# Holding the grams and the merges of inverses for a place behind a scan step on TensorE

## The chip, the cores and the metric

The kernel runs on one core of a Trainium2 chip. The metric is the device time of one execution in microseconds; the kernel before has a median of 1652.41 us over three runs. The core has five engines with a queue each: TensorE (PE, with its weight loads as PEld), VectorE (DVE), ScalarE (ACT), GpSimd (POOL) and SyncE (SP, which here only issues transfers).

## The reference

Two samples of 512 tokens and width 1024 pass through two layers with shared weights. Layer 0 is a bidirectional RWKV-7 time mixing with 16 heads of 64; layer 1 is a neighbourhood attention. Cut to what matters here:

```python
r, k, v = heads(lerp(0) @ w_r), heads(lerp(1) @ w_k), heads(lerp(2) @ w_v); z = xn @ w_z
for d in range(2):                       # forward and backward
    ...                                  # decay, a, k_d from two low-rank products
    def step(s, inp):                    # 512 steps of it, in order or reversed
        sa = einsum('bhvk,bhk->bhv', s, a_t)
        s = s * w_t + sa[..., None] * b_t + v_t[..., None] * k_t
        return s, einsum('bhvk,bhk->bhv', s, r_t)
    ys.append(scan(step, ...))
y = ys[0] + ys[1]                        # normed per head, bonus added, times silu(z), @ w_o
x = x + rms(y @ w_o)                     # then the layer of attention in the same frame
```

## The kernel before

The recurrence is done in chunks of 64 tokens (`NCH` = 8 a sequence). The work is cut into eight **blocks** (`self.todo`): two samples by four groups of four heads. For each block:

- `prep` (twice a block, for a pair of heads each, two directions d) makes the decays and the tile `ab`, and then a **gram** for each d: one bunch of 32x2 small f32 matmuls of 64x32 tiles (L975) into the bank `pf`. ScalarE copies it to Gd and Go (L981). `prep` goes on only when the gram of the direction before it has issued.
- `inverse` makes the inverse of 64x64 unit triangular matrices, 32 at a time: 32x32 halves by elimination on VectorE (L1011 transposes in, L1018 and L1020 are 30 pairs of dependent operations, L1022 masks, L1028 and L1033 transpose out to NA and MT), and then the **merges** of the halves on TensorE: two bunches of 32x32 tiles at L1049 and two at L1051, each in a bank `pm`, each followed by ScalarE copies back to NA (L1056) or MT (L1059).
- eight **scan steps** (`step`, a burst of some 55 us): states (L1186, L1192), solve and factors (L1213, L1092, L1114) and outputs (L1233, L1237), all in tiles of 64x64 or 128x64.
- `finish` norms y and stores it.

Beside the blocks runs a long list of **products** (L826 to L828): full 128x128 tiles, 24 matmuls for a column of 128 outputs, for r, v, k, z, then w_o of sample 0 (which needs the finish of sample 0's four blocks) and w_in of layer 1. Their weights and operands are split in two parts by ScalarE and VectorE (L745, L747, L771, L773).

The order of TensorE, VectorE and ScalarE in this stage is written at build time by a planner, `weave`: every activity is a thread (a generator) that yields the engine it wants next, a gate and a function `needs` that says from which time on its next piece can run. `Clock` keeps a model of the time. `weave` takes, among the threads whose time has come, the one with the lowest rank: steps 0, prep 1.5, posts 2, inverse 5, products 9. If nothing can run and TensorE has been idle, it issues a warming matmul (L1643). A thread that waits holds up itself alone, not the engine's queue. `Clock.mode` is the tile size of the last planned matmul; a change of tile size costs 100 ns in the model. The inverses are one thread, block after block:

```python
for n, (s, pb) in enumerate(self.todo):
    yield "D", lambda: did["preps"] > n and did["steps"] >= NCH * (n - 1)
    yield from self.inverse(s, pb)
    did["inverse"] += 1
```

and the second part of a step waits with `did["inverse"] > st.n`. The functions that the change touches:

Of the kernel before, what the change touches and what calls it, by code (L numbers as in the profile page):

```python
# [19 lines left out]
P = 128  # L20
# [30 lines left out]
class Clock:  # L51
# [40 lines left out]
    def room(self, key, bufs):  # L92
        s = self.slots.get(key, ())
        return 0.0 if len(s) < bufs else min(self.left(n) for n in s)

    def at(self, names):

        return max([max(self.made.get(n, {}).values(), default=0.0) for n in names], default=0.0)
# [133 lines left out]
class Trunk:  # L232
# [20 lines left out]
    NZ1, STOCK, EPS, NEAR = 4, 1, 60.0, 400.0  # L253
    HACT = (3, 4)
    WARM = 300.0
    AHEADE = dict(S=3000.0, A=200.0, D=200.0)

    def __init__(self, ctx, tc, a):
# [59 lines left out]
    def bank(self, tag="pm"):  # L318

        return (lambda: self.clock.room(tag, self.bufs[tag]) < 1e11), (lambda c: max(c.room(tag, self.bufs[tag]), 0.0))  # L320

    def dram(self, tag, shape=(P, T)):
        return self.dp.tile(list(shape), F32, tag=tag, name=self.name("d" + tag))
# [523 lines left out]
    def prep(self, s, p):  # L847
# [6 lines left out]
        need = lambda *xs: lambda c, n=[x.tensor.name for x in xs]: c.at(n)  # L854
# [33 lines left out]
        free, room = self.bank()  # L888
        for d in range(2):
# [36 lines left out]
            ab = b("ab", (P, NCH, 4, L), 1)  # L926
# [34 lines left out]
            def gram(ab=ab, d=d):  # L961

                free, room = self.bank("pf")
                yield "P", free, lambda c: max(room(c), need(ab)(c))
                ps = self.p("pf", (P, 2, T))[:, :, 0:4 * L].rearrange("p h (i t) -> p h i t", i=4)
                for i2 in range(4):
                    for par in range(2):
                        for hf in range(2):
                            for h in range(2):
                                e, i = (par + d) % 2, 2 * i2 + par  # L970
                                q = 64 * e + 32 * hf
                                rhs = ab[half(h), i, 1 if e else 2]
                                if hf:
                                    rhs = rhs.rearrange("p (b t) -> p b t", b=2)[:, ::-1]
                                nc.tensor.matmul(  # L975
                                    ps[q:q + 32, h, i2], ab[half(h), i, 3 if e else 0, 32 * hf:32 * hf + 32], rhs,
                                    start=True, stop=True, tile_position=(64 * h, q))
                yield "A", None, need(ps)
                for par in range(2):
                    e = (par + d) % 2  # L980
                    act.copy(Gd[half(e), :, par::2, g], ps[half(e), :, :, 0:32])  # L981
                    act.copy(Go[half(e), :, par::2, g], ps[half(e), :, :, 32:64])

            grams = gram()

        yield from grams
# [12 lines left out]
    def inverse(self, s, pb):  # L999

        nc = self.nc
        vt, gps, act = nc.vector, nc.gpsimd, nc.scalar
        f = lambda tag, shape: self.t(tag, shape, 1, F32, self.front)
        wc, Gd, Go = self.formed[s, pb]
        NU = 32
        free, room = self.bank()
        need = lambda *xs: lambda c, n=[x.tensor.name for x in xs]: c.at(n)
        gd, go = (x.rearrange("p h i g t -> p (h i g) t") for x in (Gd, Go))
        yield "D", None, need(Gd)
        N = f("N", (P, 32, 32))  # L1010
        vt.transpose(N, gd.rearrange("p u t -> p t u"))  # L1011
        tmp = f("etmp", (P, 256))
        self.did["gd"] += 1
        for q in range(1, 31):
            n = 31 - q
            tv = tmp[:, :n * q].rearrange("p (i j) -> p i j", i=n)
            yield "D"
            vt.tensor_tensor(tv, N[:, q + 1:, q:q + 1].broadcast_to([P, n, q]), N[:, q:q + 1, :q].broadcast_to([P, n, q]), op=ALU.mult)  # L1018
            yield "D"
            vt.tensor_tensor(N[:, q + 1:, :q], tv, N[:, q + 1:, :q], op=ALU.add)  # L1020
        yield "D"
        vt.tensor_tensor(N, N, self.lower, op=ALU.mult)  # L1022
        yield "D"
        vt.memset(N.rearrange("p i j -> p (i j)")[:, 0:1024:33], 1.0)

        yield "D"
        NA = f("NA", (P, NU, 32))
        vt.transpose(NA.rearrange("p u j -> p j u"), N.rearrange("p i j -> p j i"))  # L1028
        MT = self.MTb[self.nM % 2]
        self.nM += 1  # L1030

        yield "D"
        vt.transpose(MT[:, :, 0, :].rearrange("p u i -> p i u"), N)  # L1033
        yield "A"
        for q in (1, 3):
            r = slice(32 * q, 32 * q + 32)
            act.copy(MT[r, :, 1], MT[r, :, 0])
            gps.memset(MT[r, :, 0], 0.0)
        for step in range(2):
            for j0 in (0, 16):  # L1040
                us = slice(j0, j0 + 16)
                yield "P", free, (lambda c: max(room(c), need(NA)(c))) if step == 0 else (lambda c: max(room(c), need(MT)(c)))
                ps = self.p("pm", (P, 16, 32))
                for j in range(16):
                    for h in range(2):
                        x, y = slice(64 * h, 64 * h + 32), slice(64 * h + 32, 64 * h + 64)
                        u = j0 + j
                        if step == 0:
                            nc.tensor.matmul(ps[y, j], go[x, u], NA[x, u], start=True, stop=True, tile_position=(64 * h, 64 * h + 32))  # L1049
                        else:  # L1050
                            nc.tensor.matmul(ps[x, j], NA[y, u], MT[y, u, 1], start=True, stop=True, tile_position=(64 * h + 32, 64 * h))  # L1051
                yield "A", None, need(ps)
                for h in range(2):
                    if step == 0:
                        y = slice(64 * h + 32, 64 * h + 64)
                        act.copy(NA[y, us], ps[y])  # L1056
                    else:
                        x = slice(64 * h, 64 * h + 32)
                        act.copy(MT[x, us, 1], ps[x])  # L1059
        self.formed[s, pb] = wc, MT  # L1060
# [60 lines left out]
    def alone(self, q):  # L1121

        did, st = self.did, self.steps[q]
        free, room = self.bank("pf")
        bank, here = self.bank()
        yield (
            "P", lambda: did["factors"] > q or (did["fetch"] > q and (did["solve"] >= q if q else bank()) and free()),
            lambda c: 0.0 if did["factors"] > q else max(c.at([st.ab.tensor.name]), room(c), 0.0 if q else here(c)))
        if did["factors"] == q:
            self.factors(q)  # L1130
# [486 lines left out]
    def weave(self, threads):  # L1617

        ck, did = self.clock, self.did
        while True:  # L1620
# [5 lines left out]
            for t in ts:  # L1626
# [5 lines left out]
                else:  # L1632
                    late = max(at - max(now, ck.t[t.eng]) - self.EPS, ck.t[t.eng] - now - self.AHEADE[t.eng])
                if late <= 0:
# [3 lines left out]
                else:  # L1638
                    wake.append(now + late)
                    if t.eng == "P":  # L1640
                        soon.append(late)
            if best is None and self.spare is not None and ck.cool(now) and min(soon, default=1e9) > self.WARM:
                self.nc.tensor.matmul(self.spare, self.ident, self.scan[0][:, 0:256], start=not did["states"], stop=True, skip_group_check=True)  # L1643
# [14 lines left out]
    def scan_phase(self, mid):  # L1658
# [61 lines left out]
        def each(f):  # L1720
# [4 lines left out]
            Thread(lambda: 0, each(self.step)), Thread(lambda: 0.5, each(self.alone)), Thread(lambda: 0.5, each(self.near)),  # L1725
            Thread(lambda: 1, each(self.outer)),
            Thread(lambda: 0, fetch()), Thread(lambda: 0, fetch_x()), *self.flow(), Thread(lambda: 5, inverse()), Thread(lambda: 1.5, preps()),
            Thread(lambda: 1.3 if did["finish"] == 3 else 4, finish()), Thread(lambda: 1.2, self.norm0(0))]
        e = mybir.EngineType
# [202 lines left out]
```

## Time and profile before

| | |
|---|---|
| runs | 1654.68, 1652.41, 1652.31 us; median 1652.41 |
| the profiled execution | span 1657.8 us from the first to the last instruction; no other time of it is listed |
| PE / PEld busy | 1558.3 us (94%) / 1195.6 us (72%) |
| DVE / ACT / POOL busy | 1218.7 us (74%) / 1013.3 us (61%) / 177.9 us (11%) |
| products in this stage, L826 + L827 + L828 | 284.7 + 258.1 + 257.2 us busy |
| grams L975 / merges L1049, L1051 | 29.1 us (x2048) / 19.9 and 21.1 us (x1024 each) |
| warming matmuls L1643 | 52.9 us (x200) |

Matmuls overlap in the pipeline, so sums of busy time over groups exceed the time that they take; intervals between starts say more. In the windows view each row is a stretch of the span: its length, then for PE, PEld, DVE, ACT and POOL the busy time and the count of instructions, then the granted TensorE clock, the share of the DMA engines and GB/s; restricted to a line it shows only the engines that this line uses. In the timeline each row is a start, a time, an engine, the line, the operation, the tiles written and read, shapes and a count of merged instructions, and in brackets idle time before it with its releaser.

### The profile page before, as it was taken

What the parts mean: (1) busy time and instruction counts of PE and PEld (TensorE: products, weight loads), DVE (VectorE), ACT (ScalarE), POOL (GpSimd) and SP (SyncE); (2) the same over time, 40 slices, a digit from 0 to 9 for tenths busy, and PEclk for the clock granted to TensorE, in tenths of its full rate; (3) what the DMA queues carried; (4) which work ended last, traced back from release to release, by engine and by line L of the source; (5) the groups of instructions that cost most, each with busy time, mean ns of one, the idle gap of its engine ahead of it and who ended that gap; (6) DMA issues with size and microseconds to landing.
All of it is one profiled execution on the core that took longest, in us unless ns stands there. A gap on an engine that the chain in (4) does not pass through costs nothing.

```text
span 1657.8 us, 46551 instructions
## 1 busy us (share of the span) xinstructions
PE 1558.3 (94%) x18824; PEld 1195.6 (72%) x18824; DVE 1218.7 (74%) x2711; ACT 1013.3 (61%) x2025; POOL 177.9 (11%) x338
## 2 busy tenths in 40 slices
PE   7989888898999998988988999999999999999998
PEld 5867667676767776766766767777777778777776
DVE  8886668688789687886879887855677585665564
ACT  6567656766765677655665765354567665455562
POOL 0000213411101123000000111000000002100000
PEclk9999999999999899988988999999999999999999
DMA  5455578676687687664668665554765346745453
GB/s 212 157 174 175 183 259 283 212 233 224 211 257 253 193 265 255 220 219 162 222 218 266 205 227 188 185 178 129 286 216 179 109 140 206 246 159 182 163 163 103
DMA packets 176184, 336.29 MB, mean 203 GB/s; under 512 B 20928, under 2 KB 53824, under 8 KB 175968
## 3 DMA queue, kind: packets, MB, share of 16 engines
q1 hardware_dynamic: 152480, 253.07, 47.9%
q0 software_dynamic: 23488, 80.23, 13.7%
q8 instruction: 148, 2.42, 0.6%
q14 instruction: 68, 0.56, 0.1%
HBM read 227.71 MB, written 105.51 MB: 201 GB/s over the span
## 4 chain that ended last, share of the span: by engine, by line
PE 72%; DVE 9%; ACT 8%; DMA 6%; issue 4%; POOL 0%; SPq 0%; DVEq 0%; ACTq 0%; POOLq 0%
PE pm L826 8%; PE pg L430 6%; PE pg L431 6%; PE pg L432 6%; PE pm L827 6%; PE pm L828 6%; PE pf L1114 3%; DMA dab<-ab 2%; PE us L1233 2%; PE us L1213 2%; PE sc L1452 2%; PE zy L1186 2%; PE po L1485 2%; PE zy L1237 2%; PE pt L1470 2%
## 5 line engine op out<-in xcount | busy, mean ns | idle before, releaser
L826 PE MATMUL pm<-act,whi 128*128 128x512 f32 x640 | 284.7, 445 | 6.0 <-ACT whi L745 2.2
L827 PE MATMUL pm<-act,whi 128*128 128x512 f32 x640 | 258.1, 403 | 15.9 <-DVE act L773 13.2
L828 PE MATMUL pm<-act,wlo 128*128 128x512 f32 x640 | 257.2, 402 | 7.6 <-DVE wlo L747 7.6
L430 PE MATMUL pg<-act,whi 128*128 128x512 f32 x384 | 158.5, 413 | 0.2 <-DVE tmp L1408 0.2
L826 PEld LDWEIGHTS pm<-act,whi 128*128 128x128 f32 x640 | 122.8, 192 | 47.6 <-issue 10.5
L379 ACT CAST whi<-raw 128x512 fp32r<-128x512 f32 x148 | 91.5, 618 | 102.9 <-PE pg L431 65.7
L827 PEld LDWEIGHTS pm<-act,whi 128*128 128x128 f32 x640 | 123.4, 193 | 42.1 <-DVE act L773 18.3
L432 PE MATMUL pg<-act,wlo 128*128 128x512 f32 x384 | 152.5, 397 | 0.0
L431 PE MATMUL pg<-act,whi 128*128 128x512 f32 x384 | 152.4, 397 | 0.0
L828 PEld LDWEIGHTS pm<-act,wlo 128*128 128x128 f32 x640 | 123.5, 193 | 37.4 <-DVE wlo L747 10.1
L380 DVE TENSOR_TENSOR wlo<-raw,whi 128x512 fp32r<-128x512 f32 x148 | 101.2, 685 | 57.1 <-ACT whi L379 56.3
L747 DVE TENSOR_TENSOR wlo<-raw,whi 128x512 fp32r<-128x512 f32 x160 | 109.1, 685 | 42.9 <-ACT whi L745 41.7
L745 ACT CAST whi<-raw 128x512 fp32r<-128x512 f32 x160 | 98.2, 619 | 54.1 <-PE pm L827 35.8
L430 PEld LDWEIGHTS pg<-act,whi 128*128 128x128 f32 x384 | 72.3, 188 | 15.4 <-issue 3.3
L432 PEld LDWEIGHTS pg<-act,wlo 128*128 128x128 f32 x384 | 72.2, 188 | 14.9 <-issue 0.3
L431 PEld LDWEIGHTS pg<-act,whi 128*128 128x128 f32 x384 | 72.4, 189 | 14.0 <-issue 2.5
L1018 DVE TENSOR_TENSOR etmp<-N 128x30 f32<-128x30 f32 (+14 forms) x240 | 78.4, 326 | 4.1
L1020 DVE TENSOR_TENSOR N<-etmp,N 128x30 f32<-128x30 f32 (+14 forms) x240 | 78.4, 327 | 3.8
L1225 ACT COPY X<-us 64x256 f32<-64x256 f32 x128 | 47.0, 367 | 39.3 <-PE zy L1092 34.1
L1463 DVE CUSTOM_DVE_ANT_0 sb<-sc,bias 128x256 f32<-128x256 f32 x128 | 49.2, 418 | 28.2 <-PE pt L1470 20.6
L1466 ACT ACTIVATE sb<-sb,mx 128x256 f32<-128x256 f32 x128 | 64.2, 503 | 7.0 <-DVE mx L1465 6.7
L1114 PE MATMUL pf<-cab 64*64 64x128 f32 (+1 forms) x2048 | 67.2, 268 | 1.1 <-issue 1.1
(408 smaller groups left out, 3661.4 us busy)
## 6 DMA issues: line engine op xcount, KB each, us to landing
dab<-ab POOLq DMA_DIRECT2D x32, 1024.0 KB, 7.3
cab<-dab SPq DMA_DIRECT2D x64, 512.0 KB, 5.0
raw<-in_w_in_dram SPq DMA_DIRECT2D x128, 256.0 KB, 3.3
bias<-in_rpb_dram SPq DMA_DIRECT2D x32, 384.0 KB, 4.7
raw<-in_w_z_dram SPq DMA_DIRECT2D x32, 256.0 KB, 4.7
raw<-in_w_k_dram SPq DMA_DIRECT2D x32, 256.0 KB, 3.4
raw<-in_w_r_dram SPq DMA_DIRECT2D x32, 256.0 KB, 3.2
k<-dk SPq DMA_DIRECT2D x32, 256.0 KB, 4.2
```

The costliest lines, as they stand in the source:

```text
L379: self.nc.scalar.copy(hi, src)
L380: (eng or self.nc.vector).tensor_tensor(lo, src, hi.bitcast(F32), op=ALU.subtract)
L430: nc.tensor.matmul(ps, hi, x[k][0], start=(k == 0), stop=False)
L431: nc.tensor.matmul(ps, hi, x[k][1], start=False, stop=False)
L432: self.mm = nc.tensor.matmul(ps, lo, x[k][0], start=False, stop=(k == KT - 1))
L745: nc.scalar.copy(hi, raw[h])
L747: nc.vector.tensor_tensor(lo, raw.pop(h), hi.bitcast(F32), op=ALU.subtract)
L826: nc.tensor.matmul(ps, hi[:, at], xh, start=(k == 0), stop=False)
L827: nc.tensor.matmul(ps, hi[:, at], xl, start=False, stop=False)
L828: nc.tensor.matmul(ps, lo[:, at], xh, start=False, stop=(k == KT - 1))
L1018: vt.tensor_tensor(tv, N[:, q + 1:, q:q + 1].broadcast_to([P, n, q]), N[:, q:q + 1, :q].broadcast_to([P, n, q]), op=ALU.mult)
L1114: end = nc.tensor.matmul(st.f[half(a), h, 0, d, g] if st.last else st.f[half(a), h, :, d, g], ab[half(h), d, g, 2 * e[d] + 1 - a], rt if s ...
```

## The change

The bunches of grams (32) and of merges (32) are given a later time in the planner: as long as the last planned matmul is a full 128x128 one, the time from which the bunch may issue is put off by 4000 ns of the planner's clock. As soon as the last planned matmul is of another tile size, the bunch may issue from its old time on. No instruction is added or removed; the order on the engines changes.

```diff
+    ALONE = 4000.0
...
+    def beside(self, at):
+
+        return lambda c: at(c) + (self.ALONE if c.mode == (128, 128) else 0.0)
...
             def gram(ab=ab, d=d):
                 free, room = self.bank("pf")
-                yield "P", free, lambda c: max(room(c), need(ab)(c))
+                yield "P", free, self.beside(lambda c: max(room(c), need(ab)(c)))
...
         for step in range(2):
             for j0 in (0, 16):
                 us = slice(j0, j0 + 16)
-                yield "P", free, (lambda c: max(room(c), need(NA)(c))) if step == 0 else (lambda c: max(room(c), need(MT)(c)))
+                yield "P", free, self.beside((lambda c: max(room(c), need(NA)(c))) if step == 0 else (lambda c: max(room(c), need(MT)(c))))
```

`room` is the planner's time at which a bank comes free, `need` the time at which the tiles named are made.

## The prediction

> **What bounds the kernel now.** I first read the page's head and the table of instructions by engine, then the windows view over 186 to 1166 us (the stage in which scan steps, grams, merges and products are woven), then the timeline of one inverse. The runs lie at 1652.3 to 1654.7 us with median 1652.41; the profiled execution's span is 5.4 us above that median. Differences are summed on the span and applied to the median.
>
> ```profile
> span 1657.8 us, 46551 instructions
> PE 1558.3 (94%) x18824; PEld 1195.6 (72%) x18824; DVE 1218.7 (74%) x2711; ACT 1013.3 (61%) x2025; POOL 177.9 (11%) x338
> ```
>
> 94% busy looks like a kernel bound by TensorE, for which fewer changes of array shape would be worth something. That is an average over stages, so the next question is where the bunches to be moved stand. The windows view, cut so that scan bursts (8 steps) and the gaps between them alternate and restricted to L1051 (second half of the merges), says:
>
> ```profile
> 329.00:387.00 58.00, 0.00 (x0) 0.00 (x0) 0.99 0.78 253
> 387.00:436.00 49.00, 2.40 (x128) 2.18 (x128) 0.97 0.64 211
> ...
> 1099.00:1148.00 49.00, 0.00 (x0) 0.00 (x0) 1.00 0.53 169
> ```
>
> The eight gaps hold 128 records each (64 a bunch), the eight bursts none; gap 387 to 436 and the first and last burst are shown. Every merge stands in a gap. The reason is in the code: the step's solve waits for did["inverse"], so burst n cannot begin before the merges of block n have ended, and burst n-1 (58 us in the first row) is over before elimination n is. The timeline of block 1's merges, all engines, shows what hangs on them:
>
> ```profile
> 416.12 2.22 DVE L1028 STREAM_TRANSPOSE NA<-N 128x1024 f32<-128x1024 f32 x1
> 418.82 2.02 DVE L1033 STREAM_TRANSPOSE MT<-N 128x1024 f32<-128x1024 f32 x1
> 421.50 1.20 PE L1049 MATMUL pm<-NA,Go 32*32 32x32 f32 x64
> 422.04 1.96 POOL L1038 MEMSET MT<- 32x1024 f32 x2 [1.55 <-ACT MT L1037]
> 423.73 1.17 ACT L1056 COPY NA<-pm 32x512 f32<-32x512 f32 x2
> 426.74 1.20 PE L1049 MATMUL pm<-NA,Go 32*32 32x32 f32 x64
> ...
> 428.76 1.20 PE L1051 MATMUL pm<-MT,NA 32*32 32x32 f32 x64
> 430.00 1.17 ACT L1059 COPY MT<-pm 32x512 f32<-32x512 f32 x2 [0.85 <-PE pm L1051]
> 431.47 1.20 PE L1051 MATMUL pm<-MT,NA 32*32 32x32 f32 x64
> 433.90 1.17 ACT L1059 COPY MT<-pm 32x512 f32<-32x512 f32 x2
> 434.63 1.99 DVE L1011 STREAM_TRANSPOSE N<-Gd 128x1024 f32<-128x1024 f32 x1
> ```
>
> The last row is the first instruction of the next block's inverse: it starts 0.7 us after the last copy of this one. The inverse is one thread that goes through eight blocks in series, and bursts hang on it. This chain, not TensorE, paces the scan. Whether a longer chain costs time depends on TensorE's reserve, which the timeline shows at two places:
>
> ```profile
> 746.74 4.15 PE L1643 MATMUL zy<-cc 128*128 128x256 f32 x18
> ...
> 758.59 0.79 PE L827 MATMUL pm<-act,whi 128*128 128x512 f32 x1 [7.47 <-DVE act L773]
> ...
> 1146.85 0.70 PE L1237 MATMUL zy<-X,R 128*64 128x64 f32 x16
> 1165.56 0.39 PE L828 MATMUL pm<-act,wlo 128*128 128x512 f32 x1
> ```
>
> Before 758 us the products have run dry: TensorE issues warming matmuls (L1643) and then stands for 7.5 us, because the next products read y of sample 0, which needs burst 3 and its finish. So blocks 0 to 3 are bound by the chain without any reserve. After it the chain has some reserve: the last step ends at 1147, the last product at 1165.6. In these 18.7 us the finish and the next stage put matmuls of their own, so I take 13 us of products, between 0 and 18.7, that can fill later gaps.
>
> **What a place beside a step is worth.** Product, gram, product in the timeline; then a step before a product without and with a gram between:
>
> ```profile
> 205.85 0.39 PE L828 MATMUL pm<-act,wlo 128*128 128x512 f32 x1
> 206.17 0.86 PE L975 MATMUL pf<-ab 64*32 64x64 f32 x64
> 206.96 0.50 PE L826 MATMUL pm<-act,whi 128*128 128x512 f32 x1
> 207.30 0.40 PE L827 MATMUL pm<-act,whi 128*128 128x512 f32 x1
> ...
> 366.37 0.41 PE L1192 MATMUL zy<-V,AK 64*64 64x64 f32 x16
> 366.71 0.50 PE L826 MATMUL pm<-act,whi 128*128 128x512 f32 x1
> 367.05 0.39 PE L827 MATMUL pm<-act,whi 128*128 128x512 f32 x1
> 367.28 0.40 PE L828 MATMUL pm<-act,wlo 128*128 128x512 f32 x1
> ...
> 460.79 0.41 PE L1192 MATMUL zy<-V,AK 64*64 64x64 f32 x16
> 461.13 0.86 PE L975 MATMUL pf<-ab 64*32 64x64 f32 x64
> 461.92 0.50 PE L826 MATMUL pm<-act,whi 128*128 128x512 f32 x1
> ```
>
> Between products a gram takes 207.30 - 205.85 = 1.45 us, less two product intervals of 0.23 (367.05 to 367.28): 0.99. After a step it takes (461.92 - 460.79) - (366.71 - 366.37) = 0.79. A bunch that finds a step saves 0.20 us. The gram at 461 shows that some grams stand there already; the merges, as seen, have no step to find, and grams outside bursts none either. So I put the saving at nothing (0 to 4 us for up to 20 grams, where TensorE binds at all).
>
> **The hold, step by step.** beside() adds 4.0 us to the time from which a bunch may issue, counted from its data or bank, as long as the last matmul was full size. Where no step comes, the hold is 4.0 us less the age of the data when the thread asks. The held bunch blocks no engine's queue: products, warmers and steps issue past it. What is behind it is its own thread: for a merge its ACT copies, the next merge, then the solve and the next elimination; for a gram its copies, the key sums, the POOL store of ks, and on SP the loads of the next pair.
>
> Grams of block 0 (four), before any step:
>
> ```profile
> 186.00:329.00 143.00, 0.00 (x0) 0.00 (x0) 0.97 0.72 235
> 195.78 0.68 DVE L940 TENSOR_TENSOR ab<-kp,u 128x512 f32<-128x512 f32 x1
> 199.04 0.86 PE L975 MATMUL pf<-ab 64*32 64x64 f32 x64
> 206.02 0.69 DVE L940 TENSOR_TENSOR ab<-th,u 128x512 f32<-128x512 f32 x1
> 244.65 1.99 DVE L1011 STREAM_TRANSPOSE N<-Gd 128x1024 f32<-128x1024 f32 x1
> ```
>
> The first row is the windows view for L1186, the state matmuls of a step: none up to 329. The d=0 gram comes 2.6 us after its data (199.04 - 196.46), hold 1.4; the d=1 gram comes with its data (206.02, gram at 206.17), hold 4.0. Two pairs: 2 x 5.4 = 11 us, straight before the first inverse (244.65). Bounds 0 and 16.
>
> Grams of later blocks: block 2's preparation ended with L991 at 414.67, 19 us before its inverse began at 434.63, so 5 to 11 us of hold are covered there; without that cover they would cost 5.4 a pair.
>
> ```profile
> 414.67 0.75 DVE L991 SCALAR_TENSOR_TENSOR kp<-kp,cv,r 128x512 f32<-128x512 f32 x1
> 331.00:411.00 80.00, 74.54 (x1404) 53.03 (x1403) 68.45 (x146) 53.62 (x110) 8.64 (x16) 0.98 0.69 226
> 412.00:435.00 23.00, 22.85 (x396) 15.83 (x382) 13.42 (x19) 15.13 (x27) 4.39 (x7) 1.00 0.74 247
> 754.00:777.00 23.00, 18.41 (x300) 14.19 (x303) 11.06 (x14) 12.45 (x19) 2.41 (x3) 0.72 0.50 171
> ```
>
> Merges, per block: first L1049 asks after L1033 (ends 420.84), with NA made at 418.34, age 2.5, hold 1.5. Second L1049 needs NA, which the copies have just rewritten (end 424.90): fresh, hold 4.0. First L1051 needs MT, made by 424.0, 4.8 us old: no hold by data, but a bank of pm may have come free later; 0 to 4, I take 1, since three banks serve and one is usually long free. Second L1051 needs MT just rewritten (431.17): 4.0. Sum 10.5 us a block, bounds 8 and 16. In block 1, L670 (two columns, so not full size) comes once a column of products, 24 x 0.23 = 5.5 us, and opens the gate: a mean hold near 2.5 instead of 4, together 6. In block 0, grams of block 1 stand among the merges: 8. Blocks 0 to 3: 8 + 6 + 10.5 + 10.5 = 35; blocks 4 to 7: 42.
>
> What is given back: while merges are held TensorE works off products, whose splits then do not burden VectorE during the next elimination. The windows view shows VectorE (third figure) busy 68.45 of 80 us in elimination 1, 86%, and 13.42 of 23 in its merges, of which some 5.5 are the inverse's own (L1028 2.22, L1033 2.02, and the mask L1022, estimated at somewhat over half of one of these): other work runs at 7.9/23 = 34%. Each held microsecond moves 0.34 us of such work out of a stretch that is 86% full: 0.34/0.86 = 0.40 given back. Bounds 0 and 0.8.
>
> Sum: before y of sample 0, (11 + 35) x 0.6 = 28; after it 42 x 0.6 = 25, less the 13 of products: 12. Total +40: span 1698, median **1692 us**. Own range: with 0.8 given back 9 + 0, so 1662; with nothing given back 46 + 29, so 1728.
>
> In the row 754 to 777 the granted clock is 0.72, behind the dry stretch with its 7.47 us of idling. The Trainium skill, "TensorE: Matmul & The Clock Gate", Part 1, says that an idle window of about 3.4 us brings the clock back to half; the trace agrees. By that rule a dry stretch longer by 28 us would also slow the matmuls in it; at half speed for one block of merges (4 bunches of 1.2 us) that would add about 5 us, an estimate, and the sum would be 1697 instead of 1692.
>
> **The rivals.** (1) Faster: the planner finds a partner for most bunches and the chain does not feel the holds. 0.20 us x 53 bunches (32 merges, 21 grams) = 10.6, of which about half lies after 758 us where TensorE binds: 1647. For it: 94% busy. Against it: the x0 rows. It decides if the hold after 758 us stays under 13/0.6/4 = 5 us a block and before it near none. The Trainium skill, "TensorEngine Tiling (Array Packing)", Key Properties, has it that every change of tiling mode drains TensorE, which speaks against this rival: gram and step differ in shape (64x32, 64x64), so a pair still drains between them. The trace agrees (L1192 to L975 0.34, as L1192 to L826), and 0.20 holds that already. (2) No change: eliminations take back all of the hold, 1649 to 1656. Against it: 34% other work. (3) Worse: a bank that comes free anew renews the hold, 16 us a block and nothing given back: 16 + 128 - 13 = 131, so 1783.
>
> **How the numbers follow.** About 0.2%, 3.3 us, is what a measurement can tell from none. Forecast 0.72, rival 1 0.14, rival 2 0.08, rival 3 0.06. The range leaves out rivals 1 and 3: 1648 to 1728. Faster 0.14, same 0.08, slower 0.78.
>
> **What would show it.** In the changed kernel: L1049 to the next L1049 in a gap near 9 instead of 5.2 us; the first L1011 near 252 instead of 244.65; L1011 of successive blocks some 6 us further apart; more L1643; the last L1237 near 1190; the part after the scan as long as now. Wrong if the merges' spacing stays or if eliminations shrink as much as the merges grow.

## The result, and the profile after

The changed kernel took 1713.61 us (median of four runs, 1710.08 to 1715.57) against 1652.36 (1652.11 to 1654.68) for the kernel before on the same chip: a ratio of 1.0373, 95% interval 1.0356 to 1.0390. It is slower by 61 us; 40 were forecast. The profiled executions have spans of 1657.8 and 1708.3, which is +50.5. Before's span lies 5.4 above its median, after's 5.3 below; these two make up the rest of the 61. Below, parts are compared by the spans.

Lines behind the new function are five higher in the changed kernel: L1011 became L1016, L1022 L1027, L1049 L1054, L1051 L1056, L1056 L1061, L1237 L1242, L1279 L1284, L1643 L1648, L826 to L828 L831 to L833. The page's head, engines and warming matmuls:

```profile
span 1708.3 us, 46851 instructions
PE 1585.3 (93%) x18962; PEld 1225.5 (72%) x18962; DVE 1223.3 (72%) x2711; ACT 1012.1 (59%) x2025; POOL 177.8 (10%) x338
L1648 PE MATMUL zy<-cc 128*128 128x256 f32 x338 | 90.2, 404 | 0.7 <-ACT Z L1203 0.5
```

VectorE, ScalarE and GpSimd issue as many instructions as before; TensorE has 138 more matmuls, and there are 138 more warming matmuls (338 against 200). So the edit itself adds no instruction, but the planner filled new waits with warming matmuls: the change added no work, only time in which TensorE had none.

The windows view, cut at bursts and gaps and restricted to the second half of the merges (L1056), the second burst, the gap behind it and the last gap:

```profile
339.00:398.00 59.00, 0.00 (x0) 0.00 (x0) 1.00 0.68 224
398.00:460.50 62.50, 2.40 (x128) 2.18 (x128) 0.95 0.62 200
...
1117.00:1150.80 33.80, 2.25 (x128) 2.14 (x128) 1.00 0.58 187
```

Merges still stand in gaps alone: none of the bunches met a scan step. They only came later. Of the 32 bunches of grams, counted from the records, 14 now stand right behind other small tiles (11 behind a scan step, 3 behind merges) instead of 9. By the prediction's 0.20 us a bunch, these five are worth 1 us. The timeline of block 1's merges, the block that the prediction showed (its row of 431.09 is the first bunch, that of 449.31 the second):

```profile
421.46 2.25 DVE L1033 STREAM_TRANSPOSE NA<-N 128x1024 f32<-128x1024 f32 x1
...
427.86 1.99 DVE L1038 STREAM_TRANSPOSE MT<-N 128x1024 f32<-128x1024 f32 x1
...
431.09 1.20 PE L1054 MATMUL pm<-NA,Go 32*32 32x32 f32 x64
...
439.08 1.17 ACT L1061 COPY NA<-pm 32x512 f32<-32x512 f32 x2
...
449.31 1.20 PE L1054 MATMUL pm<-NA,Go 32*32 32x32 f32 x64
450.55 1.17 ACT L1061 COPY NA<-pm 32x512 f32<-32x512 f32 x2 [2.74 <-PE pm L1054]
451.33 1.20 PE L1056 MATMUL pm<-MT,NA 32*32 32x32 f32 x64
...
459.28 2.06 DVE L1016 STREAM_TRANSPOSE N<-Gd 128x1024 f32<-128x1024 f32 x1
```

The bunches themselves last 1.20 us as before. From the first transpose out (L1033) to the next block's inverse it is now 37.8 us, against 18.5 (416.12 to 434.63). The timeline of after has the start of the first inverse, the beginning of the finish of block 3 (y of sample 0, called y0 below), the last product and the last output of the scan; the last fence is the beginning of that finish in the timeline of before:

```profile
251.82 2.08 DVE L1016 STREAM_TRANSPOSE N<-Gd 128x1024 f32<-128x1024 f32 x1 [2.42 <-ACT Gd L986]
...
750.08 1.21 DVE L1284 TENSOR_REDUCE st<-y 128x16 f32<-128x1024 f32 x1
...
1147.70 0.39 PE L833 MATMUL pm<-act,wlo 128*128 128x512 f32 x1
1147.93 1.89 PE L1648 MATMUL zy<-cc 128*128 128x256 f32 x8
...
1204.70 0.69 PE L1242 MATMUL zy<-X,R 128*64 128x64 f32 x16
```

```profile
722.95 1.21 DVE L1279 TENSOR_REDUCE st<-y 128x16 f32<-128x1024 f32 x1
```

y of sample 0 comes 27 us later, the scan's end 58 us later, the program's end 50.5 later. And the last product is now issued 57 us ahead of the scan's end, at 1147.70, with warming matmuls right behind it; before it was issued 19 us behind the scan's end.

From y0 on, both spans are cut into four stretches: the 50 us behind it, up to the last burst (the first solve matmul of block 7), the last burst, and the rest. The windows view, all engines (the first pair of figures is TensorE's busy time and count); before, then after:

```profile
722.90:772.90 50.00, 38.20 (x433) 29.44 (x434) 35.49 (x63) 24.80 (x44) 4.48 (x7) 0.80 0.55 175
772.90:1098.20 325.30, 307.79 (x5454) 235.09 (x5455) 271.13 (x541) 197.76 (x376) 27.82 (x47) 0.97 0.64 207
1098.20:1147.30 49.10, 48.54 (x1123) 36.32 (x1124) 22.30 (x43) 21.43 (x46) 1.62 (x3) 1.00 0.54 173
1147.30:1657.80 510.50, 498.02 (x2837) 393.25 (x2832) 321.16 (x985) 291.05 (x650) 31.94 (x59) 1.00 0.54 177
```

```profile
750.10:800.10 50.00, 43.28 (x597) 32.57 (x598) 36.44 (x61) 30.99 (x54) 4.47 (x7) 0.90 0.58 185
800.10:1150.90 350.80, 337.42 (x5484) 260.01 (x5480) 282.14 (x552) 204.34 (x385) 30.52 (x52) 0.98 0.63 207
1150.90:1205.20 54.30, 44.48 (x1114) 36.27 (x1110) 18.88 (x37) 19.21 (x43) 1.62 (x3) 1.00 0.35 109
1205.20:1708.30 503.10, 478.72 (x2738) 376.93 (x2732) 311.28 (x969) 279.94 (x634) 29.25 (x54) 0.98 0.53 173
```

The same view restricted to the products' line (before L826, after L831; the last burst and what follows) and to the warming matmuls of the last two stretches of after:

```profile
1098.20:1166.00 67.80, 20.73 (x46) 8.60 (x46) 1.00 0.52 165
```

```profile
1150.90:1205.00 54.10, 0.00 (x0) 0.00 (x0) 1.00 0.35 108
```

```profile
1150.90:1205.00 54.10, 3.50 (x10) 1.49 (x10) 1.00 0.35 108
1205.00:1708.30 503.30, 6.27 (x26) 4.84 (x26) 0.98 0.53 173
```

Before, 46 matmuls of each of the three lines were left when the last burst began, 138 x 0.23 = 32 us of work; TensorE was busy in 48.5 of that burst's 49.1 us. After, none were left, and it was busy in 44.5 of 54.3.

Behind the scan one wait stands out. The next stage, the attention, begins with scores (L1452, after L1457) that need the tile k. The timeline of after, with the first scores and the third:

```profile
1235.17 2.08 PE L1457 MATMUL sc<-k,q 64*128 64x256 f32 x8 [13.16 <-DMA k<-dk]
...
1244.51 1.13 PE L1457 MATMUL sc<-k,q 64*128 64x256 f32 x8 [0.62 <-DVE mx L1468]
```

The windows view from the scan's end to the first scores, before (they start at 1182.83) and after, then the first 7.4 us of scores in after:

```profile
1147.60:1182.80 35.20, 35.20 (x155) 28.18 (x155) 21.16 (x32) 15.24 (x22) 2.70 (x5) 1.00 0.59 201
```

```profile
1205.40:1235.20 29.80, 16.64 (x76) 13.11 (x76) 12.53 (x18) 4.61 (x7) 0.00 (x0) 0.84 0.45 149
1235.20:1242.60 7.40, 6.72 (x27) 4.40 (x28) 3.25 (x19) 4.18 (x11) 0.00 (x0) 0.50 0.91 357
```

Before, 59 products and 79 matmuls of the next products (L430 to L432) filled this stretch, and no wait for k shows. After, 35 of the latter were all that was left (L435 to L437), and TensorE stood 13.16 us until k had landed.

To compare kernels I count from the records the time in which TensorE does no work: time without a matmul, a warming matmul not counted as work. I call it bare time. Between y0 and the end it is 61.3 us before and 86.8 after. The remainder, TensorE's work after y0, is 873.6 and 871.4: the same. So the end is 750.1 + 871.4 + 86.8 = 1708.3, against 722.9 + 873.6 + 61.3 = 1657.8: 27 us later to y0, 25.5 more bare, 2 less work. The extra lies in the last burst (0.6 to 12.2) and behind the scan (13.0 to 29.3); of the two stretches ahead of them the first has 6.6 less, the second 4.2 more. (Busy times of the rows give the same within 4 us; there a warming matmul that overlaps work is counted twice.)

### The profile page after: what moved, and what is told of

The parts are those of the page before. It is cut to its first block, busy times and chain, and to the rows that moved or that the text cites. A ratio compares the mean times of both kernels' runs of the same rounds, so it can differ in the third digit from the quotient of the medians.

```text
span 1708.3 us, 46851 instructions
## 1 busy us (share of the span) xinstructions
PE 1585.3 (93%) x18962; PEld 1225.5 (72%) x18962; DVE 1223.3 (72%) x2711; ACT 1012.1 (59%) x2025; POOL 177.8 (10%) x338
## 4 chain that ended last, share of the span: by engine, by line
PE 71%; DVE 11%; ACT 8%; DMA 5%; issue 4%; SPq 0%; DVEq 0%; POOL 0%; ACTq 0%
PE pm L831 8%; PE pm L832 6%; PE pm L833 6%; PE pg L435 6%; PE pg L436 6%; PE pg L437 6%; PE pf L1119 3%; PE zy L1191 2%; PE us L1238 2%; PE sc L1457 2%; PE us L1218 2%; PE po L1490 2%; PE pt L1475 2%; PE zy L1242 1%; PE zy L437 1%
## 5 line engine op out<-in xcount | busy, mean ns | idle before, releaser
L831 PE MATMUL pm<-act,whi 128*128 128x512 f32 x640 | 280.7, 439 | 16.8 <-ACT act L776 11.5
L832 PE MATMUL pm<-act,whi 128*128 128x512 f32 x640 | 257.8, 403 | 13.3 <-DVE act L778 11.6
L833 PE MATMUL pm<-act,wlo 128*128 128x512 f32 x640 | 256.8, 401 | 6.6 <-DVE wlo L752 6.6
L831 PEld LDWEIGHTS pm<-act,whi 128*128 128x128 f32 x640 | 123.0, 192 | 61.7 <-ACT act L776 15.1
L435 PE MATMUL pg<-act,whi 128*128 128x512 f32 x384 | 158.6, 413 | 0.1
L437 PE MATMUL pg<-act,wlo 128*128 128x512 f32 x384 | 152.9, 398 | 0.0
L833 PEld LDWEIGHTS pm<-act,wlo 128*128 128x128 f32 x640 | 123.3, 193 | 38.0 <-DVE wlo L752 10.9
L1648 PE MATMUL zy<-cc 128*128 128x256 f32 x338 | 90.2, 404 | 0.7 <-ACT Z L1203 0.5
L435 PEld LDWEIGHTS pg<-act,whi 128*128 128x128 f32 x384 | 72.3, 188 | 15.4 <-issue 3.3
L437 PEld LDWEIGHTS pg<-act,wlo 128*128 128x128 f32 x384 | 72.1, 188 | 14.9 <-issue 0.3
L1648 PEld LDWEIGHTS zy<-cc 128*128 128x128 f32 x338 | 65.3, 200 | 14.4 <-issue 2.8
```

The costliest lines, as they stand in the source:

```text
L435: nc.tensor.matmul(ps, hi, x[k][0], start=(k == 0), stop=False)
L437: self.mm = nc.tensor.matmul(ps, lo, x[k][0], start=False, stop=(k == KT - 1))
L831: nc.tensor.matmul(ps, hi[:, at], xh, start=(k == 0), stop=False)
L832: nc.tensor.matmul(ps, hi[:, at], xl, start=False, stop=False)
L833: nc.tensor.matmul(ps, lo[:, at], xh, start=False, stop=(k == KT - 1))
```

## Experiments

All are compared with the kernel before on the same chip. The table gives, for each, the start of the finish of block 3 ("y0"), bare time in the 50 us behind it, from there to the last burst ("middle"), and in the last burst and the rest ("end"), then TensorE's work behind y0; the five sum to the span. These columns come from one execution each, whose span lies up to 5.4 us off the median, so a few us between two rows tell nothing.

| kernel | median us | ratio [95%] | y0 | first 50 | middle | end | work |
|---|---|---|---|---|---|---|---|
| before | 1652.4 | | 722.9 | 27.1 | 20.6 | 13.6 | 873.6 |
| after | 1713.6 | 1.0373 [1.0356, 1.0390] | 750.1 | 20.5 | 24.8 | 41.5 | 871.4 |
| e1 merges held alone | 1724.2 | 1.0441 [1.0409, 1.0472] | 752.9 | 18.7 | 34.5 | 38.2 | 878.3 |
| e2 grams held alone | 1663.0 | 1.0049 [1.0024, 1.0073] | 732.1 | 18.9 | 24.9 | 13.3 | 877.1 |
| e3 hold of 1 us | 1692.8 | 1.0252 [1.0224, 1.0281] | 719.8 | 19.3 | 32.1 | 42.5 | 875.6 |
| e4 paired merges, no hold | 1680.1 | 1.0178 [1.0148, 1.0207] | 710.1 | 9.0 | 34.6 | 34.6 | 890.4 |
| e5 merges of blocks 0-3 held | 1682.2 | 1.0173 [1.0149, 1.0197] | 759.1 | 18.0 | 22.3 | 14.1 | 868.0 |
| e6 merges of blocks 4-7 held | 1703.7 | 1.0304 [1.0277, 1.0330] | 723.4 | 27.6 | 38.2 | 40.2 | 872.5 |
| e7 e4 with elimination 5 first | 1661.3 | 1.0051 [1.0028, 1.0074] | 709.2 | 8.6 | 41.9 | 10.5 | 889.9 |
| e8 elimination 5 first, alone | 1680.0 | 1.0166 [1.0138, 1.0193] | 717.1 | 27.8 | 47.6 | 10.7 | 874.3 |
| e9 hold within bursts only | 1667.6 | 1.0088 [1.0064, 1.0113] | 715.3 | 14.9 | 35.2 | 15.0 | 889.1 |
| e10 pairs in blocks 0-3 only | 1670.2 | 1.0113 [1.0084, 1.0142] | 711.6 | 9.9 | 33.6 | 21.3 | 892.0 |
| e11 pairs in blocks 4-7 only | 1646.2 | 0.9953 [0.9936, 0.9971] | 722.9 | 28.2 | 18.6 | 10.6 | 868.6 |
| e12 hold by data, not bank | 1714.6 | 1.0374 [1.0325, 1.0423] | 747.0 | 19.6 | 39.5 | 40.1 | 869.7 |

The expectations name theories by letters and say what each holds. A is the prediction's own: the eight inverses are one chain, and a microsecond of hold costs a fixed part of itself. The columns of the table were chosen after the last run; the expectations go by other quantities.

**First: which bunches, how long, and the opposite of a hold.** e1 keeps the hold at the merges and takes it from the grams; e2 the reverse; e3 sets it to 1 us (lines with a hold are those of the changed kernel, and `...` stands for code left out):

```diff
# e1: the gram as before
-                yield "P", free, self.beside(lambda c: max(room(c), need(ab)(c)))
+                yield "P", free, lambda c: max(room(c), need(ab)(c))
# e2: the merge as before
-                yield "P", free, self.beside((lambda c: max(room(c), need(NA)(c))) if step == 0 else ...
+                yield "P", free, (lambda c: max(room(c), need(NA)(c))) if step == 0 else ...
# e3
-    ALONE = 4000.0
+    ALONE = 1000.0
```

e4 has no hold and makes merges faster: both bunches of a half are issued before their copies, so the second no longer waits for the copies of the first; the second half then waits for NA too.

```diff
         for step in range(2):
+            made = []
             for j0 in (0, 16):
...
-                ... else (lambda c: max(room(c), need(MT)(c)))
+                ... else (lambda c: max(room(c), need(NA, MT)(c)))
...
+                made.append((us, ps))
...
-                yield "A", None, need(ps)
+            for us, ps in made:
+                yield "A", None, need(ps)
```

> The hold of 4 us on the merges alone; grams issue as before. Theory A (the eight inverses in series pace the scan, and each held microsecond of a merge lengthens that series by about 0.6 us): most of the loss stays, +40 to +54, so 1692 to 1706 us. Theory B (the loss is TensorE's: worse order, later operands, colder clock, in proportion to the bunches held): half the loss, about 1683 us. Theory C (any other order costs some tens of us, whatever is held): anything from 1680 to 1720, without relation to the series of inverses.

> The hold of 4 us on the grams alone; merges issue as before. Theory A: only the four grams of block 0 stand on the path, 11 us x 0.6 = +7, so 1655 to 1663 us. Theory B: half the loss, about 1683 us. Theory C: 1680 to 1720 us.

> The change with a hold of 1 us in place of 4. Theory A: the first merge of a half and the d=0 grams are older than 1 us when they ask, so 2 us a block remain on the merges and 2 us on the grams of block 0: 18 x 0.6 = +11, less what products at the end take up, 1653 to 1663 us. Theory B: a quarter of the loss, about 1667 us. Theory C: as with 4 us, 1690 to 1720 us.

> The kernel before, without any hold, but both bunches of a merge half are issued before their copies to SBUF, so that a round trip from TensorE to ScalarE and back goes from each half. Theory A: the series of inverses is shorter by some 6 us a block, x 0.6, which counts in full before y of sample 0 (-14) and little after it: 1630 to 1644 us. Theory B: the bunches and changes of tile size on TensorE are as many, no gain: 1648 to 1656 us. Theory C: slower by tens of us, 1670 or more.

The hold of merges is the costly part: e1 alone costs 70 us, more than the whole change's 61; e2 costs 8. The parts don't add up (78), which is the first sign that the cost is not a sum of holds. At y0 theory A holds: +30 in e1, +9 in e2, and the pairs of e4 bring it 13 earlier. The ends contradict it. e3 has y0 3 us earlier than before and still loses 38; e4 gains 13 at y0 and loses 26. Both lose behind y0. Of the expectations, A's alone met e2, C's alone met e3 and e4, and e1 came out slower than all three had it.

**Second: halves of the scan, and a collision.** e5 holds merges of sample 0 (blocks 0 to 3) only, e6 those of sample 1 only:

```diff
+                yield "P", free, (self.beside if s == 0 else (lambda f: f))((lambda c: ...
# e6: s == 1
```

In e4 the residual sum of layer 0 (L781, on VectorE), which w_in's products wait for, had moved into elimination 5, which grew to 134.5 us from 102.2 before. The planner gives the residual rank 0.6 and the inverse rank 5. e7 is e4 with that one elimination ranked ahead of the residual; e8 is the kernel before with the same rank:

```diff
-Thread(lambda: 5, inverse())
+Thread(lambda: 0.55 if did["inverse"] == 5 else 5, inverse())
```

> The 4 us hold on the merges of blocks 0 to 3 alone (grams free, blocks 4 to 7 free). Theory A (each held microsecond lengthens the series of inverses; products at the end cover a little): the finish of block 3 comes 21 to 30 us later and the rest is as long as before, 1675 to 1685 us. Theory D (before y of sample 0 as A, but after it what counts is where layer 0's residual, some 30 us of VectorE work, falls: beside the merges of block 5, as in the kernel before, or inside elimination 5): the stretch from the finish of block 3 to the end is either as before (935 us) or 25 to 35 us longer, so 1675 to 1685 or 1700 to 1720 us.

> The 4 us hold on the merges of blocks 4 to 7 alone. Theory A: +12, the finish of block 3 stays at 723 us, 1660 to 1668 us. Theory D: the finish of block 3 stays, the stretch behind it is longer by 20 to 35 us, 1675 to 1690 us. If the effects add, this loss and that of the hold on blocks 0 to 3 make up the 70 us of the hold on all merges.

> The paired merges (no hold) with one thing more: while block 5 is inverted, the inverse thread has rank 0.55, ahead of the residual (0.6), so that elimination 5 no longer waits for it on VectorE. Theory D: elimination 5 falls from 134 us to some 95, and the time from 1680 to 1640-1660 us. Theory A gives the collision no weight: no change from 1680 us, give or take 5.

> The control: the kernel before with rank 0.55 for the inverse thread while block 5 is inverted, no hold. Theory D: elimination 5 lost little to the residual there, so 0 to -15 us, 1638 to 1655 us. Theory A: elimination 5 is part of the series, some 10 us shorter, of which the products at the end let half through: 1645 to 1652 us. If products starve behind the late residual: 1660 us or more.

e5's time lies in A's range and in the first of D's, but by two misses that cancel. Its finish of block 3 begins 36 us later, where 21 to 30 were expected, and from there to the end it is not as long as before, but 12.5 us shorter on the spans (6 by the medians):

```profile
759.07 1.21 DVE L1284 TENSOR_REDUCE st<-y 128x16 f32<-128x1024 f32 x1
```

e6 leaves y0 in place and costs 51 us: far above A's figure, which was a price per held microsecond less a cover, and above D's. Of its extra bare time of 45 us, 27 lies at the end and 18 in the middle. So a hold on the merges of blocks 0 to 3 moves y0, and one on those of blocks 4 to 7 opens the loss at the end. e5 and e6 together make +81, e1 +70: the two don't simply add.

The residual and elimination 5 did meet in e4. Six of the residual's eight operations by the view of their line (count, shortest, median and longest in ns, first and last start), and elimination 5 by the windows view (from its first transpose to its mask), in e4 and then in e7:

```profile
L781 DVE SCALAR_TENSOR_TENSOR xr<-xr,cv,acc x6: 731/746/749, 837.9 to 897.4; 128x512 f32<-128x512 f32 x6
```

```profile
778.40:912.90 134.50, 120.41 (x1798) 91.45 (x1793) 110.77 (x220) 79.13 (x153) 7.90 (x15) 0.95 0.68 220
```

```profile
L781 DVE SCALAR_TENSOR_TENSOR xr<-xr,cv,acc x6: 743/748/754, 864.4 to 928.6; 128x512 f32<-128x512 f32 x6
```

```profile
777.90:824.50 46.60, 42.46 (x1011) 32.30 (x1003) 36.03 (x97) 22.31 (x48) 0.12 (x1) 0.93 0.41 124
```

With its rank raised, the elimination takes 46.6 us instead of 134.5, and the kernel is 19 us faster, just above D's range and well off A's. Not all of the 88 us is the residual's: the rank puts this elimination ahead of preparations and splits too, and before, with 5 us of the residual's stretch inside, it took 102.2. The table says where the time went: end 34.6 to 10.5, while the middle rises (34.6 to 41.9), where the residual comes some 30 us later and w_in's products wait for it. Why the end gains is not separated. Inverse 6 starts later than in e4 (939.52 instead of 927.04) and inverse 7 at the same time (1037.95, 1037.58), so the shorter elimination did not reach the chain behind it; but 144 products instead of 48 were left for the last burst and the stretch behind it, as a late residual would leave them. In e8 there was little collision to cure, and the other effect is left: middle 20.6 to 47.6, 28 us lost, as the last branch of its expectation had it.

**Third: a hold with hardly any place, and pairs in halves.** e9 holds only while a burst is under way, when steps do come; e10 and e11 pair the bunches in the blocks of one sample only:

```diff
# e9
-        return lambda c: at(c) + (self.ALONE if c.mode == (128, 128) else 0.0)
+        return lambda c: at(c) + (self.ALONE if c.mode == (128, 128) and self.did["steps"] % NCH else 0.0)
# e10, e11: the loop of e4 under this test, else the loop of before
+        if s == 0:      # e11: s == 1
```

> The change with one condition more: the 4 us are added only while a burst of steps runs (the count of finished steps is no multiple of 8), so that no bunch is held where no step can come. Merges then issue as before, and only grams that ask inside a burst wait for a step. Theory A (holds cost only on the series of inverses): 1648 to 1656 us, with at most 4 us from saved changes of tile size. Theory D (the balance after y of sample 0 can tip with any shift): 1645 to 1690 us.

> The paired merges for blocks 0 to 3 alone, no hold. Theory A: the finish of block 3 at 710 instead of 723 us, and the rest as in the kernel before: 1638 to 1646 us. Theory D: the rest is longer again because layer 0's residual then falls into elimination 5: 1665 to 1685 us, as with all merges paired.

> The paired merges for blocks 4 to 7 alone, no hold. Theory A: the series after block 3 is some 20 us shorter, of which TensorE, full there, lets through a third at most: 1643 to 1652 us. Theory D: the finish of block 3 as before, 723 us; the merges of block 5 end before the residual is through, so it falls into an elimination: 1660 to 1685 us.

e9 holds where steps do come, and does not gain: it is 0.9% slower (A had 1648 to 1656), with 14.6 us more bare time in the middle. e9 and e10 have y0 8 and 11 us earlier, but then 15 to 18 us more work stands behind it: products that were done ahead of y0 before were not done yet. So an advance of y0 gained nothing in these runs (e4 and e7 have 16 to 17 us more work as well), while most of a delay stayed: y0 and the work behind it are together 25 us later in after, for 27 at y0, and 31 in e5, for 36. e10 ended in D's range, e11 in A's. e11 changes only the later blocks, and is the fastest of all: 1646.2, faster than before by 0.47% (0.29 to 0.64). Its last burst, by the windows view:

```profile
1090.60:1139.30 48.70, 48.69 (x1127) 36.62 (x1126) 24.85 (x47) 22.20 (x47) 1.62 (x3) 1.00 0.57 178
```

TensorE is busy all through it, and the middle has only 18.6 bare. Which of the moved operations gained the 0.47% was not tested.

**Fourth: what renews a hold.** In after, the second bunch of block 7 came 11.5 us behind the first. Timeline:

```profile
1124.95 1.20 PE L1054 MATMUL pm<-NA,Go 32*32 32x32 f32 x64
...
1128.69 1.17 ACT L1061 COPY NA<-pm 32x512 f32<-32x512 f32 x2
...
1128.93 1.02 PE L1307 MATMUL pm<-ks,cc 128*128 128x512 f32 x2
...
1130.48 0.60 PE L1317 MATMUL pm<-cc,y 128*128 128x128 f32 x4
...
1132.35 0.74 DVE L1320 SCALAR_TENSOR_TENSOR bv<-pm,dv,bv 128x512 f32<-128x512 f32 x1
...
1136.50 1.20 PE L1054 MATMUL pm<-NA,Go 32*32 32x32 f32 x64
```

Its data was there at 1129.9. Meanwhile two full-size bunches took banks `pm`, one came free when L1320 had read it (1133.1), and 3.4 us later the bunch was issued. That fits a hold counted anew from the bank. e12 counts it from the data alone:

```diff
-self.beside(lambda c: max(room(c), need(ab)(c)))
+lambda c: max(room(c), self.beside(need(ab))(c))
# and the same for both halves of the merges
```

> The whole change, but the 4 us are counted from the data alone; a bank of PSUM that comes free anew no longer renews the hold. If renewed holds are what made the merges of blocks 4 to 7 grow by 68 us (from the end of elimination to the last copy, 94 to 162) where 42 were expected: they grow by 35 to 50 here, the merges of block 7 in particular fall from 38 to about 33 us, and the time is 1685 to 1702 us. If not (the copies and the queue on ScalarE stretched them): as the change, 1708 to 1718 us, with the merges of blocks 4 to 7 near 160.

From the mask to the next block's inverse, blocks 4 to 6 take 118.6 us in after, 82.8 in e12 and 68.7 before. Of the 36 us between after and e12, 22 lie ahead of the end of the second transpose out, on VectorE, where no hold acts (in after the residual stands there in block 5); 14 are left for the bunches, and that is the most that the renewal can account for. The time does not move (1.0374 and 1.0373), which the expectation had for the case that the renewal is not the cause, though the merges did get shorter. The three eliminations of these blocks take 250.2 us in after and 303.3 in e12, and its residual lies in elimination 5 (its line's view, then the windows view):

```profile
L786 DVE SCALAR_TENSOR_TENSOR xr<-xr,cv,acc x6: 742/744/748, 870.4 to 913.0; 128x512 f32<-128x512 f32 x6
```

```profile
806.60:933.60 127.00, 116.27 (x1722) 89.81 (x1721) 112.69 (x223) 78.14 (x152) 8.42 (x16) 0.99 0.74 241
```

**What the fourteen traces say together.** Behind y0 two losses come and go separately. In the middle, bare time is 19 to 25 us where at most 12 us of the residual's stretch (from its first operation to its last) lie inside elimination 5 (before, after, e2, e5, e11), and 32 to 40 where 29 us or more of it do (e3, e4, e6, e9, e10, e12); the exceptions are e1, 34.5 with 11 us inside and long held merges behind, and e7 and e8, where the residual was put off by rank. At the end, bare time is 11 to 15 us where at least 132 products were left for the last burst and after it, 21 with 96, and 35 to 43 with 48 or fewer. The wait for k goes with it: 12.1 to 13.2 us in the six with 48 or fewer (after, e1, e3, e4, e6, e12), 5.6 in e10, none in the other seven. In those six the first scores start 29 to 30 us behind the scan's end each time, with 35 matmuls of the next products, the finish and warming to fill them. Of the 21 to 29 us that their ends lose against before, about 17 lie there and the rest in the last burst. The two patterns are read from traces; no run tests each cause by itself. In particular, what tipped e3 (a hold of a quarter) into both losses stays open: any edit lets the planner choose anew.

## Why the prediction was right, and where its size was off

- **The chain of inverses paces the scan, and no merge finds a step: right.** The x0 rows stayed, and e5, with no other hold than that on the merges of blocks 0 to 3, moved y0 by 36 us and the end by 24 on the spans (30 on the medians).
- **Nothing saved beside a step: right as far as it shows.** e2 and e9, the two in which a hold had most chance to meet steps at little cost to the merges, are slower by 0.49% and 0.88%. Five more grams stand behind small tiles in after, 1 us by the prediction's own price, within its 0 to 4. Rival 1 (1647) is out: its condition, a hold under 5 us a block behind y0, was not met either.
- **Grams of block 0, 11 us of hold, 7 on the path: right.** The first inverse starts at 251.82 instead of 244.65, +7.2; e2 has +9 there. One reading was off: 206.02 is the start of that L940, which ends at 206.71, so the rows do not give the age of the d=1 gram's data.
- **Merges of blocks 0 to 3, 35 of hold, 21 after give-back: near in sum, by luck, with wrong parts.** From the first inverse to that of block 4 it is 441.5 us instead of 416.2, +25.3. The merges' part grew by 23.2, not 35: 44 more in blocks 0 to 2, and 21 less in block 3. The eliminations grew by 2.1: up to there nothing was given back, against my 0.40. y0 came 27.1 later, for 28 forecast.
- **Merges of blocks 4 to 7, 42 of hold, 25 on the path: near in sum, by luck again.** In blocks 4 to 6 the merges' part grew by 50 and the eliminations shrank by 47.5, which leaves +2.5. But 30 of the 47.5 is elimination 4, which stands ahead of the merges of block 4. It has no splits of products in after (L747 and L773; 14 of them before) and half the preparation (8 of L940 instead of 16). It is as short in e5, where only blocks 0 to 3 are held, and as long as before in e6: a give-back from the earlier holds. In e6, where only blocks 4 to 7 are held, nothing is given back: from inverse 4 to inverse 7 the merges take 28 us more and the eliminations 10 more. Block 7 has +22.9 to the scan's end, of which only some 11 is its merges; elimination 7 has 6.7 and the last burst 5.2. Rival 3 had the renewal of a hold by a bank, but with nothing given back (1783); by e12 the renewal does not set the time.
- **"Less the 13 of products": the step that failed.** I took products at the end as a free reserve, since TensorE could do them in earlier gaps. It did: TensorE's work behind the scan fell by 24 us (510.5 less 13.0 bare, against 503.1 less 29.3). But these products had covered the finish and the wait for k at the start of the next stage, and without them 16 us of bare time opened there, 13.16 of it in that one wait. The stretch shrank by 7.4, not 13, and the last burst, without products beside it, went from 49.1 to 54.3 us. By the forecast's own terms: chain 53 forecast, 57.8 measured; cover 13 and 7.4; so +50.5 instead of +40 by the spans. The other 10.7 of the 61 is where the two profiled executions stand to their medians.
- **Rival 2, no change (eliminations take all back): out.** In after, the +2.5 of blocks 4 to 6 looks like it, but e6 shows that holds there are not taken back: inverse 7 starts 37.6 us later in it.
- **The clock behind the dry stretch.** The 50 us behind y0 have a granted clock of 0.90 instead of 0.80, and bare time fell from 27.1 to 20.5: this stretch did not get drier. The 5 us that the rule of the Trainium skill, "TensorE: Matmul & The Clock Gate", Part 1, would have added (1697) did not come there. The trace agrees with the rule elsewhere: behind the 13.16 us without a matmul the granted clock is 0.50 for 7.4 us, and the eight matmuls of scores take 2.08 us, against 1.13 nine us later. That loss, 4 us at most by the half clock over 7.4 us (an estimate), is in no term of the forecast.
- **What would show it.** First inverse near 252: yes. L1054 to the next L1054 "near 9 instead of 5.2": 24.4, 18.2, 5.9, 5.2, 13.7, 8.6, 8.0 and 11.5, mean 11.9 against a mean of 7.7; block 1's 5.2, which I took for all, was at the low end. Inverses of successive blocks 6 us further apart: +4.0 on the mean, but between -12 and +14 each. Last output near 1190: 1204.7. The part behind the scan as long: 7 us shorter, though 13 us of products were to leave it, and that is where the forecast missed most.

## What to carry to other kernels

When a wait is put into a serial chain, its cost is decided at the next point where a stock of work is released (here y0): most of a delay up to there stayed (31 of 36 us in e5), and an advance gained nothing. Behind it, write the end as a start plus the bound engine's work plus its bare time, stretch by stretch: work that "fills gaps earlier" is no reserve if it covers a wait where it lies now, so look for the first wait behind the stock (here that for k) before counting on it. And merges, which found no step in the trace of before (x0 rows), found none by waiting. Pairing the bunches in the later blocks (e11) was worth 0.5%; pairing them in the earlier ones too (e4) cost 1.8%.

## What the runs showed that was not expected

No surprise of the chip itself: bunches, transposes and copies kept their lengths (1.20, 2.0 to 2.3, 1.17 us). The surprise was how much the order is worth: with the same instructions but for warming matmuls, and with holds that hardly find a place (e9) or are a quarter as long (e3), bare time behind y0 went from 61 to 65 and 94 us.
